# A hybrid encoder block on one core: both mixer projections with tokens stationary, some of their blocks by seven products instead of eight

## The chip, the core and the metric

The kernel runs on one core of a Trainium2 chip. The core has a matrix engine (TensorE, PE in the rows, with weight loads PEld), a vector engine (VectorE, DVE), a scalar engine (ScalarE, ACT), a general engine (GpSimd, POOL) and a sync engine (SyncE, SP) that here only issues DMAs. Each engine takes its instructions in program order. The metric is the device time of one execution in microseconds, the median of several.

## The reference

256 tokens of width 4096 go through two sub-layers, in fp32. Cut to what matters:

```python
h = rmsnorm(x, g_pre)
proj = h @ w_in                                   # 4096 x 12288
q, k, v, gate_a, u_b, gate_b = split(proj)        # widths 2048 each
y_a = chunked_rel_attention(q, k, v) * silu(gate_a)          # 16 heads of 128
y_b = multiscale_pool(u_b, w_pool, pool_scale) * silu(gate_b)  # 4 groups of 512
x = x + rmsnorm(concat(y_a, y_b) @ w_out, g_post)            # 4096 x 4096
h = rmsnorm(x, g_xa_pre); m = rmsnorm(mem, g_mem)            # 256 memory tokens
q, k, v = h @ w_xq, m @ w_xk, m @ w_xv            # widths 1024, 4 heads of 256
x = x + rmsnorm(softmax(q @ k.T) @ v @ w_xo, g_xa_post)
```

`w_in` and `w_out` are three quarters and one quarter of the mixer's weights, 256 MB in fp32, and by far the most of the arithmetic.

## The kernel before, in words

**Precision.** Every fp32 operand is split in two fp32r parts, a high part (a rounded copy) and a low part (the difference). A product is made of three: high by high, low by high, high by low.

**The stream.** All weights come in one list of *subs* (`stream_order`, L43), tiles of 128 partitions x 1024 columns in fp32, 512 KB each. `load_sub` (L155) brings a sub into one of 4 `raw` buffers. `split_sub` (L162) makes its high part with a copy on ACT (L174) and its low part with a subtraction on DVE (L175), into one of 4 ring buffers. The main loop (L939) takes one sub per iteration *i*, which this document calls slot *i*: first the steps listed for the slot's start, then `split_sub` of sub i+3, the DMA of sub i+7, the other steps listed for the slot (`at(i, f)` puts f there), then the matmuls of sub *i*. So everything is issued in the order of this list, on each engine's own queue, and a step that waits holds up all that stands behind it on its engine.

**Two forms of matmul.** In *column form* (`mm_cols`, L274, lines L277 and L278) a 128 x 128 block of weights is stationary and the 256 tokens move: one matmul of 512 columns (high and low tokens side by side) with the high weights, one of 256 with the low weights. The result has features on partitions. In *strip form* (`mm_strip`, L280, lines L286 to L288) 128 tokens are stationary and 512 weight columns move: three matmuls of 512 for each half of the tokens, with tokens on partitions in the result. Before the change v (a quarter of the columns of group A) and the cross-attention's v are in strip form; q, k, both gates, the pool input and w_out are in column form; the cross-attention's k (`mm_xk`, L290) is in column form with 256 moving columns.

**Around the matmuls.** The first 16 slots also build xHL, the split input (`x_prep`, L321). A column result is gathered from PSUM by a copy on ACT and an addition on DVE (L298). For each head there are steps at set slots after the end of its k columns: `head_qk_split`, `head_scores`, `head_max`, `head_exp`, `head_soft`, `head_turn` (transposes on PE, L414), `head_turned`, `head_att`, `head_y`. The gates use an exponential on ACT and a reciprocal on DVE. There are 8 PSUM banks; a product in progress holds one, a v strip two. PE is given its next sub as soon as both parts of it are there.

The DMA queue of SP carries all weights; PSUM banks are taken and given back in a fixed order by `bank` and `done` (L119, L125).

Of the kernel before, what the change touches and what calls it, by code (L numbers as in the profile page):

```python
# [36 lines left out]
XV_REST = 24  # L37
XO_HEAD = 6
OUT_HEAD = 4
# [3 lines left out]
def stream_order():  # L43
# [14 lines left out]
    subs = []  # L58
    for hg in range(4):
        subs += [strip("v", hg, k) for k in range(0, KT, 2)]  # L60
        for h in range(4 * hg, 4 * hg + 4):
            for c in (h, 16 + h, 48 + h):
                subs += cols("in", c)
    xv = [strip("xv", 0, k) for k in range(0, KT, 2)]
    for g in range(4):
        for j, c in enumerate([64 + 4 * g + j for j in range(4)] + [80 + 4 * g + j for j in range(4)]):
            subs += cols("in", c)
            if j % 2 if g else j == 7:
                subs.append(xv.pop(0))
        if g < 3:  # L70
            subs += pool(g)
    subs += xv
    for k in (0, 4):
        for c in range(0, OUT_HEAD, 2):
            subs += [[("out", c + j, k + i) for j in range(2) for i in range(4)]]
    for k in range(8, KT, 8):
        if k == 16:
            subs += pool(3)
        subs += [[("out", c, k + i) for i in range(8)] for c in range(OUT_HEAD)]
    for c in range(OUT_HEAD, KT):  # L80
        subs += cols("out", c)
    for k in range(0, KT, 2):
        subs += [[("xk", k)], [("xk", k + 1)]]
        if k < XV_REST:
            subs += [strip("xv", 1, k)]
    for c in range(8):
        subs += cols("xq", c)
    subs += [strip("xv", 1, k) for k in range(XV_REST, KT, 2)]
    for k in (0, 4):
        for c in range(0, XO_HEAD, 2):  # L90
            subs += [[("xo", c + j, k + i) for j in range(2) for i in range(4)]]
    for c in range(XO_HEAD, KT):
        subs += [[("xo", c, i) for i in range(8)]]
    return subs
# [3 lines left out]
def block_kernel(ctx: ExitStack, tc: tile.TileContext, x, mem, ws, relb, vecs, out):  # L98
    nc = tc.nc
    subs = stream_order()  # L100
    n = len(subs)
    LA = 3
    WB = LA + 1
    RAWB = 4
    XB = 3
# [3 lines left out]
    big = ctx.enter_context(tc.tile_pool(name="big", bufs=1))  # L109
    wpool = ctx.enter_context(tc.tile_pool(name="wpool", bufs=1))  # L110
    xin = ctx.enter_context(tc.tile_pool(name="xin", bufs=XB))
    com = ctx.enter_context(tc.tile_pool(name="com", bufs=1))
    psum = ctx.enter_context(tc.tile_pool(name="psum", bufs=1, space=bass.MemoryType.PSUM))
# [26 lines left out]
    def halves(name):  # L140
        t = [big.tile([P, 16, 512], F32R, tag=f"A{j}", name=f"{name}{j}") for j in range(2)]

        def part(kt, k=1):
            return t[kt // 16][:, kt % 16:kt % 16 + k, :]

        return part

    def pairs(ap):
        return ap.rearrange("p (a b) -> p a b", b=S)


    raws, Hs, Ls = {}, {}, {}
    held = {}

# [6 lines left out]

    def split_sub(s, cuts=1):  # L162
        if s >= n:
            return
        r = raws.pop(s)
        if s in held:
            h, l = held[s]()
        else:
            h = wpool.tile([P, SUB], F32R, tag="wh", name="wh", bufs=WB)
            l = wpool.tile([P, SUB], F32R, tag="wl", name="wl", bufs=WB)  # L170
        w = SUB // cuts
        for j in range(cuts):
            c = slice(j * w, j * w + w)
            nc.scalar.copy(h[:, c], r[:, c])  # L174
            nc.vector.tensor_sub(l[:, c], r[:, c], h[:, c].bitcast(F32))  # L175
        Hs[s], Ls[s] = h, l

    def load_x(src, c, store, tag, eng=None):
        store[c] = xin.tile([P, 2, S], F32, tag=tag, name=tag, bufs=XB)
        (eng or nc.sync).dma_start(store[c], src[c])  # L180

    def split_act(dst, src, g):

        nc.scalar.activation(dst[:, :S], src, AF.Copy, scale=g)
        nc.vector.scalar_tensor_tensor(dst[:, S:], src, g, dst[:, :S].bitcast(F32), op0=OP.mult, op1=OP.subtract)


    class Rms:


        def __init__(self, name):
            self.name = name
            self.acc = None

        def square(self, src):

            if self.acc is None:
                self.acc = buf("acc", [P, 2, S], f"acc_{self.name}")
                nc.scalar.activation(self.acc, src, AF.Square)
                self.sq = None  # L200
            else:
                self.sq = buf("sq", [P, 2, S], "sq", bufs=2)[:, :src.shape[1], :]
                nc.scalar.activation(self.sq, src, AF.Square)

        def add(self):
            if self.sq is not None:
                nc.vector.tensor_add(self.acc, self.acc, self.sq)
                self.sq = None

        def sums(self, src=None, first=True, last=True):  # L210
            if first:
                self.p = bank("ms")
            src = self.acc if src is None else src
            for t in range(2):
                for j in range(src.shape[1]):
                    nc.tensor.matmul(self.p[:, t:t + 1], src[:, j, t * P:(t + 1) * P], ones[:, 0:1],
                                     start=first and t + j == 0, stop=last and j == src.shape[1] - 1,
                                     skip_group_check=True)

        def root(self):  # L220
            v = const.tile([P, 2], F32, name=f"v_{self.name}")
            nc.vector.tensor_scalar(v, self.p[:, 0:2], 1.0 / D, EPS, op0=OP.mult, op1=OP.add)
            done(self.p)
            self.r = const.tile([P, 2], F32, name=f"r_{self.name}")
            nc.gpsimd.tensor_tensor(out=self.r, in0=v, in1=half, op=OP.pow)
            self.dg = buf("dg", [P, 2, P], "dg")
            nc.vector.tensor_mul(self.dg, ident[:, None, :].to_broadcast([P, 2, P]),
                                 self.r[:, :, None].to_broadcast([P, 2, P]))

        def spread(self):  # L230
            self.q = bank("mr")
            nc.tensor.matmul(self.q[:, :S], ones, self.dg.rearrange("p a b -> p (a b)"), start=True, stop=True)

        def keep(self):
            self.R = buf("R", [P, S], f"R_{self.name}", bufs=2)
            nc.scalar.copy(self.R, self.q[:, :S])
            done(self.q)

        def all_at(self, i):
# [3 lines left out]
            at(i + 2, self.spread)  # L243
            first_at(i + 3, self.keep)


    class HalfRms:
# [5 lines left out]
        def sums(self, src, first, last):  # L253
            if first:
                self.p = bank("ms")
            for j in range(src.shape[1]):
                nc.tensor.matmul(self.p[:, 0:1], src[:, j, :], ones[:, 0:1], start=first and j == 0,
                                 stop=last and j == src.shape[1] - 1, skip_group_check=True)

        def root(self):  # L260
            v = const.tile([P, 1], F32, name=f"v_{self.name}")
            nc.vector.tensor_scalar(v, self.p[:, 0:1], 1.0 / D, EPS, op0=OP.mult, op1=OP.add)
# [3 lines left out]
            self.dg = buf("dg", [P, 2, P], "dg")[:, 0, :]  # L266
            nc.vector.tensor_scalar(self.dg, ident, r[:, 0:1], None, op0=OP.mult)

        def spread(self):
            self.q = bank("mr")  # L270
            nc.tensor.matmul(self.q[:, :P], ones, self.dg, start=True, stop=True)


    def mm_cols(acc, H, L, kk, X, first, last):  # L274

        w = slice(kk * P, kk * P + P)
        nc.tensor.matmul(acc, H[:, w], X, start=first, stop=last, skip_group_check=True)  # L277
        nc.tensor.matmul(acc[:, :S], L[:, w], X[:, :S], start=False, stop=last, skip_group_check=True)  # L278

    def mm_strip(accs, H, L, kk, X, first, last):  # L280

        w = slice(kk * 512, kk * 512 + 512)
        for t in range(2):
            xh = X[:, t * P:(t + 1) * P]
            xl = X[:, S + t * P:S + (t + 1) * P]
            nc.tensor.matmul(accs[t], xh, H[:, w], start=first, stop=False)  # L286
            nc.tensor.matmul(accs[t], xl, H[:, w], start=False, stop=False)  # L287
            nc.tensor.matmul(accs[t], xh, L[:, w], start=False, stop=last)  # L288

    def mm_xk(accs, H, L, X, first, last):  # L290
        for j in range(8):
            o = accs[j // 2][:, (j % 2) * S:(j % 2) * S + S]
            w = slice(j * P, j * P + P)
            nc.tensor.matmul(o, H[:, w], X[:, :S], start=first and j % 2 == 0, stop=False, skip_group_check=True)  # L294
            nc.tensor.matmul(o, H[:, w], X[:, S:], start=False, stop=False, skip_group_check=True)  # L295
            nc.tensor.matmul(o, L[:, w], X[:, :S], start=False, stop=last, skip_group_check=True)  # L296

    def gather(acc, dst):  # L298

        t = buf("t1", [P, S], "t1", bufs=2)  # L300
        nc.scalar.copy(t, acc[:, S:])  # L301
        nc.vector.tensor_add(dst, acc[:, :S], t)
        done(acc)

    accs = {}
    where = {}
    for i, s in enumerate(subs):
        for t in s:
# [8 lines left out]

# [713 lines left out]
```

## Time and profile before

| | |
|---|---|
| median of 3 runs | 1890.54 us (1890.3 to 1892.93) |
| the profiled execution | 1891.73 us |
| its span, first to last instruction | 1889.9 us |
| mean granted TensorE clock | 0.995 |
| busy: PE, DVE, ACT | 1868.0, 1221.1, 896.5 us |
| weights and inputs moved | 366.83 MB, 194 GB/s |

The sum of a profile is made against the profiled execution's own time, 1891.73, of which 1889.9 lie between its first and last instruction. A timeline row gives the start of an instruction, its length, the engine, the line, and what it writes and reads; the length of one matmul is longer than the distance to the next, since they are pipelined, so the distance of starts is the price. The same holds for DVE and ACT in a smaller measure. In square brackets stands how long the engine was idle before, and what it waited for.

### The profile page before, as it was taken

To read this page: it belongs to the slowest core of one execution; us is meant where nothing else is said; L and a number is where in the kernel's file an instruction comes from. 1 tells how busy PE (TensorE), PEld (TensorE's weight loads), DVE (VectorE), ACT (ScalarE), POOL (GpSimd) and SP (SyncE) were. 2 spreads that over 40 slices of the span, in tenths; PEclk is the share of its full clock that TensorE was granted. 3 is DMA by queue.
4 is the path that set the end of the run, shared out by engine and by line. 5 is a ranking of instruction groups with operands and counts; after the bars stand their busy time and mean duration, and the time that the engine had idled before them with its cause. 6 is when DMAs were issued, how large, how long until landed. Compare 5 with 4: busy or idle time off the path is not lost.

```text
span 1889.9 us, 27452 instructions
## 1 busy us (share of the span) xinstructions
PE 1868.0 (99%) x10732; PEld 1633.7 (86%) x10732; DVE 1221.1 (65%) x1654; ACT 896.5 (47%) x1277; POOL 11.2 (1%) x16
## 2 busy tenths in 40 slices
PE   9999999999999999999999999999999999999995
PEld 7888888888888888888888888888888899988885
DVE  8566556655665666585867678755555569955686
ACT  8444444444444444444444446544444456634551
POOL 0000000000000000000000000000000000000001
PEclk9999999999999999999999999999999999999997
DMA  8555555555555555556655556555555567755452
GB/s 303 197 195 184 188 190 191 183 190 189 185 186 192 188 184 188 184 184 211 200 201 195 192 196 209 189 190 192 190 190 190 191 232 253 243 177 181 165 190 90
DMA packets 114226, 366.83 MB, mean 194 GB/s; under 512 B 11952, under 2 KB 22320, under 8 KB 114096
## 3 DMA queue, kind: packets, MB, share of 16 engines
q1 hardware_dynamic: 111328, 363.50, 57.9%
q8 instruction: 84, 1.38, 0.3%
q10 hardware_dynamic: 2768, 1.57, 0.3%
q14 instruction: 46, 0.38, 0.1%
HBM read 360.83 MB, written 4.19 MB: 193 GB/s over the span
## 4 chain that ended last, share of the span: by engine, by line
PE 98%; DVE 1%; DMA 0%; ACT 0%; POOL 0%; issue 0%; ACTq 0%; SPq 0%; DVEq 0%; POOLq 0%
PE acc L277 50%; PE acc L278 25%; PE va L288 2%; PE va L286 2%; PE vb L286 2%; PE vb L287 2%; PE vb L288 2%; PE va L287 2%; PE xk L294 2%; PE xk L296 2%; PE xk L295 2%; PE acc L884 1%; DVE y L834 0%; PE xs L671 0%; PE xat L713 0%; DVE y L840 0%
## 5 line engine op out<-in xcount | busy, mean ns | idle before, releaser
L175 DVE TENSOR_TENSOR wl<-raw,wh 128x1024 fp32r<-128x1024 f32 (+1 forms) x645 | 788.5, 1223 | 634.6 <-ACT wh L174 633.5
L174 ACT CAST wh<-raw 128x1024 fp32r<-128x1024 f32 (+1 forms) x645 | 676.8, 1049 | 912.0 <-PE acc L277 652.1
L277 PE MATMUL acc<-xHL,wh 128*128 128x512 f32 x2560 | 900.5, 397 | 0.0
L278 PE MATMUL acc<-xHL,wl 128*128 128x256 f32 x2560 | 714.9, 279 | 0.0
L277 PEld LDWEIGHTS acc<-xHL,wh 128*128 128x128 f32 x2560 | 481.1, 188 | 112.9
L278 PEld LDWEIGHTS acc<-xHL,wl 128*128 128x128 f32 x2560 | 482.8, 189 | 0.6
L277 PE MATMUL acc<-yHL,wh 128*128 128x512 f32 x1024 | 355.5, 394 | 0.0
L278 PE MATMUL acc<-yHL,wl 128*128 128x256 f32 x1024 | 283.9, 277 | 0.0
L277 PEld LDWEIGHTS acc<-yHL,wh 128*128 128x128 f32 x1024 | 192.1, 188 | 44.7
L278 PEld LDWEIGHTS acc<-yHL,wl 128*128 128x128 f32 x1024 | 192.4, 188 | 0.1
L277 PE MATMUL acc<-h2HL,wh 128*128 128x512 f32 x256 | 91.2, 401 | 0.0
L294 PE MATMUL xk<-mhl,wh 128*128 128x256 f32 x256 | 72.5, 283 | 0.0
L296 PE MATMUL xk<-mhl,wl 128*128 128x256 f32 x256 | 72.2, 282 | 0.0
L295 PE MATMUL xk<-mhl,wh 128*128 128x256 f32 x256 | 72.1, 282 | 0.0
L278 PE MATMUL acc<-h2HL,wl 128*128 128x256 f32 x256 | 71.6, 280 | 0.0
L277 PE MATMUL acc<-xoHL,wh 128*128 128x512 f32 x192 | 67.0, 395 | 0.0
L301 ACT COPY t<-acc 128x256 f32<-128x256 f32 x160 | 57.2, 364 | 3.6 <-PE acc L278 3.6
L277 PEld LDWEIGHTS acc<-h2HL,wh 128*128 128x128 f32 x256 | 48.1, 188 | 11.4
L447 DVE RECIPROCAL ge<-ge 128x256 f32<-128x256 f32 x32 | 56.1, 1753 | 1.1
L278 PE MATMUL acc<-xoHL,wl 128*128 128x256 f32 x192 | 53.3, 277 | 0.0
L286 PE MATMUL va<-wh,xHL 128*128 128x512 f32 x128 | 51.0, 398 | 0.5 <-ACT wh L174 0.4
L288 PE MATMUL va<-wl,xHL 128*128 128x512 f32 x128 | 50.2, 392 | 0.5 <-DVE wl L175 0.5
(202 smaller groups left out, 1804.2 us busy)
## 6 DMA issues: line engine op xcount, KB each, us to landing
raw<-ws_dram SPq DMA_DIRECT2D x647, 512.0 KB, 3.3
min<-mem_dram SPq DMA_DIRECT2D x36, 256.0 KB, 3.7
xin<-x_dram SPq DMA_DIRECT2D x31, 256.0 KB, 3.9
rb<-relb_dram SPq DMA_DIRECT2D x16, 192.0 KB, 3.5
out_dram<-y SPq DMA_DIRECT2D x3, 512.0 KB, 3.0
out_dram<-y SPq DMA_DIRECT2D x4, 256.0 KB, 3.0
out_dram<-y ACTq DMA_DIRECT2D x3, 256.0 KB, 2.2
raw<-ws_dram SPq DMA_DIRECT2D x2, 256.0 KB, 4.7
```

Source lines behind the costliest of these rows:

```text
L174: nc.scalar.copy(h[:, c], r[:, c])
L175: nc.vector.tensor_sub(l[:, c], r[:, c], h[:, c].bitcast(F32))
L277: nc.tensor.matmul(acc, H[:, w], X, start=first, stop=last, skip_group_check=True)
L278: nc.tensor.matmul(acc[:, :S], L[:, w], X[:, :S], start=False, stop=last, skip_group_check=True)
L286: nc.tensor.matmul(accs[t], xh, H[:, w], start=first, stop=False)
L287: nc.tensor.matmul(accs[t], xl, H[:, w], start=False, stop=False)
L288: nc.tensor.matmul(accs[t], xh, L[:, w], start=False, stop=last)
L294: nc.tensor.matmul(o, H[:, w], X[:, :S], start=first and j % 2 == 0, stop=False, skip_group_check=True)
L295: nc.tensor.matmul(o, H[:, w], X[:, S:], start=False, stop=False, skip_group_check=True)
L296: nc.tensor.matmul(o, L[:, w], X[:, :S], start=False, stop=last, skip_group_check=True)
L301: nc.scalar.copy(t, acc[:, S:])
L447: nc.vector.reciprocal(e, e)
```

## The change

**Pairs and quads.** All of w_in and w_out is now computed with tokens stationary. A *pair* is two strips of 512 columns: A0 to A3 (v and gate of a head group), B0 to B3 (q and k), U0 to U3 (pool input and gate) and O0 to O3 (w_out). The stream runs A0, B0, A1, B1, ..., U0 to U3, O0 to O3. A *quad* is two k tiles of 128 by the two strips, two subs; a pair has 16 quads, 32 slots. Slots 0 to 31 are A0, 32 to 63 B0, 64 to 95 A1.

**Seven products.** In a quad the four token blocks (two halves of the tokens by two k tiles) and the four weight blocks of 128 x 512 form a 2 x 2 block product, 8 block products of 3 matmuls, 24 in all. In 6 of the 16 quads of each pair but A0, B0 and O0 (`FAST`, `DIRECT`) it is done with seven block products of sums and differences, 21 matmuls. The weight differences (T3, b12-b11, T2, T4) are made on DVE for each such quad; the token sums are made once, by `x_forms` for w_in and `y_forms` for w_out. The seven results stay in PSUM over a pair, in seven banks P1 to P7, and are put together at its end by `early`, `late1` and `late2`. Direct quads of such a pair add into the same banks.

**Turning.** Results now have tokens on partitions. Those which must have features there (both gates, q, k, pool input, w_out's output) are turned by `turn`, 4 transposes on PE and a copy on ACT.

**Also.** The ring has 5 buffers instead of 4. x is read twice: once in the first 16 slots for A0, and again for `x_forms`, at slots 19 to 41. The mixer's output goes out to DRAM by `y_store` and comes back for `y_forms`. Gates use a tanh instead of exponential and reciprocal. xk is in strip form with turned results, the first half of xv is computed beside it, the second after xq. The statistics of w_out's output are made by ACT with an accumulating square. The tail's moving operands are copied to contiguous tiles first.

The diff's core:

```diff
+PAIRS = ([p for g in range(4) for p in (("A", g), ("B", g))] + [("U", g) for g in range(4)]
+         + [("O", m) for m in range(4)])
+DIRECT = (("A", 0), ("B", 0), ("O", 0))
+FAST = (4, 6, 8, 10, 12, 14)
...
-    WB = LA + 1
+    WB = 5
...
+    def piece(src, cuts=1, to=None):
...
+            A.copy(h[:, c], src[:, c])
+            V.tensor_sub(l[:, c], src[:, c], h[:, c].bitcast(F32))
+        return h, l
...
     def split_sub(s, cuts=1):
-        if s >= n:
+        while waiting:
+            waiting.pop(0)()
+        if s >= n or (fast(s) and meta[s][2] == 0):
             return
...
+        r1, r2 = raws.pop(s - 1), raws.pop(s)
+        b11, b12, b21, b22 = r1[:, :512], r1[:, 512:], r2[:, :512], r2[:, 512:]
+        t3, t2, t4 = tt[:, 0:512], tt[:, 512:1024], tt[:, 1024:1536]
+        V.tensor_sub(t3, b22, b12)
+        V.tensor_sub(b12, b12, b11)
+        w = Hs[s - 1] = {}
+        w["b2"] = piece(r2)
+        w["b1"] = piece(r1)
+        V.tensor_sub(t2, b22, b12)
+        V.tensor_sub(t4, b21, t2)
+
+        def rest():
+            w["t3"] = piece(tt[:, 0:1024])
+            w["t4"] = piece(t4)
+        waiting.append(rest)
...
+    def mm_block(acc, xs, w, first, last):
+
+        T_.matmul(acc, xs[0], w[0], start=first, stop=False)
+        T_.matmul(acc, xs[1], w[0], start=False, stop=False)
+        T_.matmul(acc, xs[0], w[1], start=False, stop=last)
...
+        if o in FAST:
+            if half == 0:
+                return (("P2", "A12", ("b2", 0)), ("P3", "S4", ("b2", 1)), ("P1", "A11", ("b1", 0)),
+                        ("P5", "S1", ("b1", 1)))
+            return ("P7", "S3", ("t3", 0)), ("P6", "S2", ("t3", 1)), ("P4", "A22", ("t4", 0))
...
+    def turn(pair, k, dst, scale=1.0):
+
+        src, p = result(pair)[k], bank("tn")
+        for c in range(4):
+            T_.transpose(p[:, c * P:(c + 1) * P], src[:, c * P:(c + 1) * P], ident)
...
+    def x_forms(c):
+        src = xch.pop((1, c))
...
+            V.scalar_tensor_tensor(ft[:, a:b, :], tiles(src[:, j, :]), gv[:, G_MIX_PRE + k:G_MIX_PRE + k + 1], R,
+                                   op0=OP.mult, op1=OP.mult)
...
+        if c in FAST:
+            sums_of(ft[:, 6, :], ft[:, 7, :], ft[:, 0, :], ft[:, 1, :], ft[:, 2:6, :])
+        else:
+            q = ft[:, :6, :].rearrange("p (k f) b -> p k f b", f=3)
+            V.tensor_sub(q[:, :, 2, :], q[:, :, 0, :], q[:, :, 1, :])
+        split_copy(h, l, ft[:, :u, :])
...
+        i = first + (3 * c) // 2
+        at(i - 3, load_x, c, 1)
+        at(i, x_forms, c)
...
+        e = end_slot["A", hg]
+        at(e + 2, a_gates, hg)
+        at(e + 3, a_keep, hg)
+        e = end_slot["B", hg]
+        at(e + 1, b_turn, hg, 0)
+        at(e + 2, b_turn, hg, 1)
+        for j in range(4):
+            h, o = 4 * hg + j, e + 4 + 7 * j
+            at(o - 3, head_bias, h)
+            at(o - 1, head_qk_split, h)
+            at(o, head_scores, h)
+            first_at(o + 1, head_max, h)
+            at(o + 2, head_exp, h)
+            at(o + 3, head_soft, h)
+            at(o + 5, head_turn, h)
+            at(o + 6, head_turned, h)
+            at(o + 8, head_att, h)
+            at(o + 9, head_y, h)
```

In the rows of instructions below, a row is the line, the operation, what it writes and reads, and the size; x2 means twice in a row. `wl` and `wh` are low and high parts of weights, `tt` holds T2 to T4, `ahl` and `aql` the split keys, probabilities and queries of a head, `x_80` and `x_81` scratch tiles (probabilities, bias), `sc` scores, `ft` the token forms, `e_u_73` and `e_u_74` two results of a pair.

DVE around the scores of a head, before (the head's k and q are split between two weight tiles):

```order
L355 TENSOR_TENSOR qk<-t_778,R_x 128x256
L175 TENSOR_TENSOR wl<-raw,wh 128x1024
L338 TENSOR_TENSOR ahl<-qk,ahl 128x256
L338 TENSOR_TENSOR ahl<-qk,ahl 128x128
L175 TENSOR_TENSOR wl<-raw,wh 128x1024 x3
L391 SCALAR_TENSOR_TENSOR pr<-sc,rb 128x384
```

DVE at the same step of the second head, in the second pair A1, after (slots 74 to 76):

```order
L204 TENSOR_TENSOR tt<-raw 128x512
L205 TENSOR_TENSOR raw<-raw 128x512
L186 TENSOR_TENSOR wl<-raw,wh 128x1024 x2
L209 TENSOR_TENSOR tt<-raw 128x512
L210 TENSOR_TENSOR tt<-raw,tt 128x512
L225 TENSOR_TENSOR ahl<-pt,ahl 128x256
L225 TENSOR_TENSOR ahl<-k,ahl 128x256
L225 TENSOR_TENSOR aql<-q,aql 128x128
L186 TENSOR_TENSOR wl<-tt,wh 128x1024
L186 TENSOR_TENSOR wl<-tt,wh 128x512
L186 TENSOR_TENSOR wl<-raw,wh 128x1024
```

The split of the head's operands now stands behind all the differences and two of the pieces of a coming fast quad.

DVE after the first results, before (the split of v lies between weight tiles):

```order
L227 TENSOR_TENSOR dg<-ident,r_x 128x256
L175 TENSOR_TENSOR wl<-raw,wh 128x1024 x4
L338 TENSOR_TENSOR vhl<-v,vhl 128x512
L175 TENSOR_TENSOR wl<-raw,wh 128x1024
L302 TENSOR_TENSOR t_684<-acc,t_685 128x256
```

DVE at slots 33 and 34, after:

```order
L186 TENSOR_TENSOR wl<-raw,wh 128x1024 x2
L550 SCALAR_TENSOR_TENSOR ft<-tt,gv,x_80 128x256 x2
L398 TENSOR_TENSOR ft<-ft 128x128
L399 TENSOR_TENSOR ft<-ft 128x128
L400 TENSOR_TENSOR ft<-ft 128x128
L401 TENSOR_TENSOR ft<-ft 128x128
L225 TENSOR_TENSOR Fa_77<-ft,Fa_77 128x896
L225 TENSOR_TENSOR extra<-ft,extra 128x128
L510 SCALAR_TENSOR_TENSOR e_u_73<-x_80,e_u_73 128x512
L510 SCALAR_TENSOR_TENSOR e_u_74<-x_80,e_u_74 128x512
```

The last two rows are the gates of A0, which PE turns at slot 35; a fast form of x stands directly ahead of them.

PE at the same head's scores, before:

```order
L277 MATMUL acc<-xHL_115,wh 128x512
L278 MATMUL acc<-xHL_115,wl 128x256
L383 MATMUL sc<-qk 128x128
L376 MATMUL sc<-ahl 128x256
L377 MATMUL sc<-ahl 128x256
L378 MATMUL sc<-ahl 128x256
L277 MATMUL acc<-xHL_115,wh 128x512
```

PE at slots 74 and 75, after:

```order
L321 MATMUL P_1596<-wh,Fb_79 128x512
L322 MATMUL P_1596<-wh,Fb_79 128x512
L323 MATMUL P_1596<-wl,Fb_79 128x512
L621 MATMUL sc<-k,q 128x128
L615 MATMUL sc<-ahl,aql 128x256
L616 MATMUL sc<-ahl,aql 128x256
L617 MATMUL sc<-ahl,aql 128x256
L321 MATMUL P_1584<-wh,Fb_79 128x512
```

The four matmuls of the scores stand between the products of two subs, as before; the products are now three matmuls of 512 per bank.

## Rows read from the trace of the kernel before

**Rows 1.** The page: busy time and instructions by engine; then the chain by line.

```profile
PE 1868.0 (99%) x10732; PEld 1633.7 (86%) x10732; DVE 1221.1 (65%) x1654; ACT 896.5 (47%) x1277; POOL 11.2 (1%) x16
...
PE acc L277 50%; PE acc L278 25%; PE va L288 2%; PE va L286 2%; PE vb L286 2%; PE vb L287 2%; PE vb L288 2%; PE va L287 2%; PE xk L294 2%; PE xk L296 2%; PE xk L295 2%; PE acc L884 1%; DVE y L834 0%; PE xs L671 0%; PE xat L713 0%; DVE y L840 0%
```

**Rows 2.** Groups by form: line engine op names shapes, busy us, mean ns, idle before.

```profile
L277 PE MATMUL acc<-xHL,wh 128*128 128x512 f32 x2560 | 900.5, 397 | 0.0
...
L277 PE MATMUL acc<-yHL,wh 128*128 128x512 f32 x1024 | 355.5, 394 | 0.0
```

**Rows 3.** Timeline of PE, two stretches of column matmuls of w_in.

```profile
100.24 0.40 PE L277 MATMUL acc<-xHL,wh 128*128 128x512 f32 x1
...
105.79 0.40 PE L277 MATMUL acc<-xHL,wh 128*128 128x512 f32 x1
...
299.92 0.40 PE L277 MATMUL acc<-xHL,wh 128*128 128x512 f32 x1
...
300.98 0.40 PE L277 MATMUL acc<-xHL,wh 128*128 128x512 f32 x1
```

**Rows 4.** Timeline of PE, strip form, one slot of twelve matmuls apart.

```profile
590.07 0.39 PE L286 MATMUL va<-wh,xHL 128*128 128x512 f32 x1
...
592.79 0.39 PE L286 MATMUL va<-wh,xHL 128*128 128x512 f32 x1
```

**Rows 5.** Timeline of PE, xk, three matmuls apart.

```profile
1600.03 0.28 PE L294 MATMUL xk<-mhl,wh 128*128 128x256 f32 x1
...
1600.39 0.28 PE L294 MATMUL xk<-mhl,wh 128*128 128x256 f32 x1
```

**Rows 6.** Timeline of PE, the transposes of one head and the matmuls behind.

```profile
98.18 0.49 PE L414 MATMUL pt<-ident,pr 128*128 128x128 f32 x3
98.43 0.47 PE L277 MATMUL acc<-xHL,wh 128*128 128x512 f32 x1
98.74 0.28 PE L278 MATMUL acc<-xHL,wl 128*128 128x256 f32 x1
```

**Rows 7.** Groups by form: the weight tiles on DVE and ACT.

```profile
L175 DVE TENSOR_TENSOR wl<-raw,wh 128x1024 fp32r<-128x1024 f32 x643 | 787.1, 1225 | 632.8 <-ACT wh L174 631.7
...
L174 ACT CAST wh<-raw 128x1024 fp32r<-128x1024 f32 x643 | 675.6, 1051 | 910.2 <-PE acc L277 652.1 <-issue 116.8 <-PE vb L287 104.1
```

**Rows 8.** Timeline of DVE while it has no wait.

```profile
33.93 0.69 DVE L207 TENSOR_TENSOR acc_x<-acc_x,sq 128x512 f32<-128x512 f32 x1
34.53 0.88 DVE L185 SCALAR_TENSOR_TENSOR xHL<-xin,gv,xHL 128x256 fp32r<-128x256 f32 x2
35.33 1.22 DVE L175 TENSOR_TENSOR wl<-raw,wh 128x1024 fp32r<-128x1024 f32 x1
36.46 0.69 DVE L207 TENSOR_TENSOR acc_x<-acc_x,sq 128x512 f32<-128x512 f32 x1
```

**Rows 9.** Timeline of ACT and DVE: hand-offs between the engines.

```profile
590.04 1.05 ACT L174 CAST wh<-raw 128x1024 fp32r<-128x1024 f32 x1 [1.67 <-PE vb L287]
...
101.37 1.05 ACT L174 CAST wh<-raw 128x1024 fp32r<-128x1024 f32 x1 [1.75 <-PE acc L277]
...
102.45 1.23 DVE L175 TENSOR_TENSOR wl<-raw,wh 128x1024 fp32r<-128x1024 f32 x1 [0.24 <-ACT wh L174]
103.60 0.42 DVE L338 TENSOR_TENSOR ahl<-pt,ahl 128x256 fp32r<-128x256 f32 x1
...
104.05 0.27 ACT L420 COPY ptc<-pt 128x128 f32<-128x128 f32 x1 [1.36 <-DVE ahl L338]
```

**Rows 10.** Windows near the end: us, PE busy (matmuls), PEclk, DMA share, GB/s.

```profile
1867.00:1868.00 1.00, 0.89 (x8) 1.00 0.00 0
1868.00:1869.00 1.00, 0.00 (x0) 1.00 0.59 179
1869.00:1869.50 0.50, 0.00 (x0) 1.00 1.14 346
...
1870.00:1870.50 0.50, 0.00 (x0) 0.50 0.05 11
```

More of the change, by code (lines that the diff above doesn't have):

```diff
@@ L72, in stream_order, with put @@
[L72 to L81, printed above, removed]
+    subs, meta = [], []
+    def put(new):
+        subs.extend(new)
+        meta.extend([None] * len(new))
@@ L82, in stream_order @@
+    for i, pair in enumerate(PAIRS):
+        kind = "out" if pair[0] == "O" else "in"
+        n1, n2 = strips(pair)
+        for o in range(QUADS):
+            if o == LEAD and i and PAIRS[i - 1][0] == "U":
+                put(pool(PAIRS[i - 1][1]))
+            for half in range(2):
+                subs.append([(kind, c, 2 * o + half) for c in n1 + n2])
+                meta.append((pair, o, half))
     for k in range(0, KT, 2):
-        subs += [[("xk", k)], [("xk", k + 1)]]
-        if k < XV_REST:
-            subs += [strip("xv", 1, k)]
+        put([[("xk", k)], [("xk", k + 1)], strip("xv", 0, k)])
@@ L162, in split_sub, with fast @@
+    def fast(s):
+        m = s < n and meta[s]
+        return m and m[0] not in DIRECT and m[1] in FAST
     def split_sub(s, cuts=1):
-        if s >= n:
+        while waiting:
+            waiting.pop(0)()
+        if s >= n or (fast(s) and meta[s][2] == 0):
             return
[L165 to L180, printed above, removed]
-    def split_act(dst, src, g):
-        nc.scalar.activation(dst[:, :S], src, AF.Copy, scale=g)
-        nc.vector.scalar_tensor_tensor(dst[:, S:], src, g, dst[:, :S].bitcast(F32), op0=OP.mult, op1=OP.subtract)
+        if not fast(s):
+            Hs[s], Ls[s] = piece(raws.pop(s), cuts, held.get(s))
+            return
@@ L205, in add, with sums @@
         def add(self):
             if self.sq is not None:
-                nc.vector.tensor_add(self.acc, self.acc, self.sq)
+                a = pairs(self.acc)
+                V.tensor_add(a, a, self.sq)
                 self.sq = None
[L210 to L213, printed above, removed]
+        def sums(self):
+            self.p = bank("ms")
+            src = pairs(self.acc)
@@ L214, in sums @@
             for t in range(2):
[L215 to L220, printed above, removed]
+                for j in range(2):
+                    T_.matmul(self.p[:, t:t + 1], src[:, j, tok(t)], ones[:, 0:1], start=t + j == 0, stop=j == 1,
+                              skip_group_check=True)
@@ L290, in mm_xk @@
[L290 to L302, printed above, removed]
+        T_.matmul(acc, H[:, w], X, start=first, stop=last, skip_group_check=True)
@@ new lines, in block_kernel, with mm_pair @@
+    left = {}
+    for pair in PAIRS:
+        for o in range(QUADS):
+            for half in range(2):
+                for k, _, _ in products(pair, o, half):
+                    left[pair, k] = left.get((pair, k), 0) + 1
+    open_banks = {}
+    def mm_pair(i):
+        pair, o, half = meta[i]
+        if fast(i):
+            w = Hs[i - half]
+            if half:
+                del Hs[i - half]
+        else:
+            w = Hs.pop(i), Ls.pop(i)
+        for k, xname, wn in products(pair, o, half):
+            key = pair, k
+            start = key not in open_banks
+            if start:
+                open_banks[key] = bank(k)
+            left[key] -= 1
+            if fast(i):
+                h, l = w[wn[0]]
+                wn = wn[1]
+            else:
+                h, l = w
+            c = slice(512 * wn, 512 * wn + 512)
+            mm_block(open_banks[key], unit(pair, o, half, xname), (h[:, c], l[:, c]), start, left[key] == 0)
@@ new lines, in block_kernel @@
+    for g in range(4):
+        e = end_slot["U", g]
+        at(e + 1, pool_u, g)
+        i = [e + 2, e + 4]
+        for b in range(2):
+            for j in range(g + 1):
+                at(i[b], pool_sum, g, b, j)
+            at(i[b] + 1, pool_d, g, b)
+        at(e + 6, pool_gates, g)
+        at(e + 7, pool_turn, g)
+        for c in range(4):
+            j = end("pool", g, c)
+            at(j + 1 + c % 2, pool_y, g, c)
+            at(j + 3 + c % 2, y_store, 16 + 4 * g + c, "sg", c)
@@ new lines, in block_kernel, with x2, o_turn, o_sq @@
+    for c in range(QUADS):
+        i = slot[("O", 0), c, 0] - 3
+        at(i - 4, load_y, c)
+        at(i, y_forms, c)
+    x2t = []
+    ssq = const.tile([P, 2, 8], F32, name="ssq")
+    def x2(k, m=1):
+        return x2t[k // 4][:, k % 4:k % 4 + m, :]
+    def o_turn(m, s):
+        if m == 0 and s == 0:
+            x2t.extend(buf(f"X{j}", [P, 4, S], f"x2_{j}") for j in range(8))
+        for t in range(2):
+            turn(("O", m), f"c{t + 1}{s + 1}", x2t[2 * m + s][:, :, tok(t)])
+    def o_sq(m, s):
+        for t in range(2):
+            b = result(("O", m))[f"c{t + 1}{s + 1}"]
+            A.activation(b, b, AF.Square, accum_out=ssq[:, t, 2 * m + s:2 * m + s + 1])
```

846 lines of the change are left out of this document (485 added, 361 removed).

## Prediction

> **What bounds the kernel now.** I read the page first, then stretches of TensorE's (PE) timeline, then what VectorE (DVE) and ScalarE (ACT) take for one weight tile, and last the end of the program. PE is busy for 1868.0 of 1889.9 us, and three quarters of the chain that ended last lie in its two column-form lines L277 and L278; DVE is busy for 65% and ACT for 47% [rows 1]. So a matmul fewer is time saved for as long as DVE and ACT keep up, and any wait that the change puts before PE is time lost. DVE and ACT sit waiting today: ACT's copies wait for PE to give ring buffers back, DVE's subtractions wait for ACT [rows 7]. That slack, about 1.5 us in each 2.72 us slot, is what the change spends.
>
> The profiled execution took 1891.73 us, its span 1889.9. I make the sum on it and subtract 1.2 us at the end, since the median of the runs is 1890.54.
>
> **What PE saves.** A column unit (128 of k by 128 columns) is one 512-wide and one 256-wide matmul. Sixteen units run from 100.24 to 105.79 us, 0.347 each; three near a head's work from 299.92 to 300.98, 0.353 [rows 3]; w_in has both kinds, w_out, with little beside it, I take at 0.347. In token-stationary form twelve matmuls of 512 run from 590.07 to 592.79, 0.2267 each [rows 4]. The column units number 2560 for w_in and 1024 for w_out [rows 2], and v has 768 strip matmuls (4 strips of 32 k tiles, 6 each). Today that work takes 2560 x 0.350 + 1024 x 0.347 + 768 x 0.2267 = 1425 us. After it there are 16 pairs x 16 quads x 24 = 6144 matmuls, less 3 in each of 78 fast quads (13 pairs x 6): 5910, x 0.2267 = 1340. **-85 us**: the 234 that fall away are 53 of it, the change of form 32. Bounds: -64 if the new matmuls run at 0.229, which a busier DVE and ACT could bring, and all columns at 0.347; -93 with the columns of w_in at 0.353.
>
> xk goes from 768 matmuls of 256 at 0.12 (three in 0.36, [rows 5]), 92 us, to 384 of 512 at 0.2267, 87: **-4** (0 to -5). The tail's contiguous operands I cost at nothing.
>
> **What PE gets on top.** 56 turned results and 4 of xk need 4 transposes each, 240. Three of today's take 98.18 to 98.43, and the matmul behind them takes 0.31 instead of 0.23 [rows 6]: 0.33 per three, and (4 x 0.083 + 0.08) = 0.41 per four, 60 x 0.41 = **+25** (20 to 30).
>
> So PE alone would come to 1889.9 - 85 - 4 + 25 = 1826. The rest is waits that do not exist today.
>
> **Weight preparation of a fast quad.** DVE issues a 512-wide operation every 0.60, a 1024-wide one every 1.13 and two scaled subtractions of 256 in 0.80 [rows 8]. A fast quad needs four differences of 512 and pieces of 1024, 1024, 1024 and 512: 4 x 0.60 + 3 x 1.13 + 0.60 = 6.4 us, where a direct quad needs 2.26. A fast and a direct quad together: 8.7 us of DVE for 45 matmuls, 10.2 us of PE. Alone this fits, and I cost it at nothing. The 1.5 us of cover is gone wherever DVE has something else to do; the next four terms are those places.
>
> **x_forms, +11.** x is read again and built into forms at slots 19 to 41, one every 1.5 slots, while A0 and B0 run direct. A plain form takes 0.80 (two scalings), 0.33 (a 256 subtraction), then DVE stands still until ACT has copied 768 columns (about 0.9 with the hand-off: copy to subtraction is 1.08 for 1024, [rows 9]), then 0.87: 3.0. A fast form takes 3.9 (four more 128-wide sums). Iterations 19 to 33 hold 7 plain and 3 fast forms and 15 pieces: 21 + 11.7 + 17 = 49.7 us against 15 x 2.72 = 40.8 of PE: DVE falls 8.9 behind. In iteration 34 the gates of A0 (two 512-wide operations) stand behind a piece and a fast form, 6.3 us. With five ring buffers DVE starts iteration 19 about 1.3 us after PE starts slot 18. So the gates end 1.3 + 8.9 + 6.3 = 16.5 us after PE would start slot 33; PE wants to turn them at slot 35, 5.4 after it. Queued behind that turn are all the matmuls of slot 35. Wait: 11 (2 if ACT's copies cost DVE nothing, 14 with wider hand-offs). Later pieces are in time again.
>
> **Attention in the fast zone, +37.** The work of a head group runs during the next pair, four times (A1, A2, A3, U0) across its fast quads, on in-order queues. Seven banks are held by products, so scores, transposes and outputs of a head share the eighth. I count from PE's start of the first fast quad in A1. PE would end its next three slots at 2.7, 5.1 and 7.8, and then do head 1's scores. DVE's piece for the slot of the scores can begin only when PE gives a ring buffer back in the first slot: ACT at 1.3, DVE 2.4 to 3.5 [rows 9]. Then come two differences, two pieces, two differences, to 8.3, and only behind them the low halves of k, q and the transposed probabilities, each after an ACT copy that itself waits for DVE (1.4 us of such waiting stands between DVE and ACT today already, in the last of rows 9): 9.9 instead of 8.2, wait 1.7. Then head 0's output waits for head 1's maximum, which frees the bank; the maximum stands behind a piece whose buffer PE gives back at the end of the slot before: ACT 12.7, DVE 13.8 to 15.0, maximum 15.5, PE free at 12.8: 2.8. By the same count head 1's output waits 2.4 behind T4, head 3's scores 2.2, the rest under 0.3 each. 9.1 per pair, x 4 = **+37**. Bounds: 4 per pair if only the two outputs wait, a little less each, 13 if each of the eight scores and outputs waits: 16 to 52.
>
> **Pool and y_forms, +10.** In U1, U2 and U3 three banks of the fast quads become free only after pool_y of the group before, about 2 us each: +6 (0 to 9). In O0 the sums of the last pool group and 16 y_forms (DVE 1.9 to 3.4 per two slots) come on top of the pieces; pool_turn waits behind them: +4 (0 to 10). The y stores and loads through DRAM are 256 KB each on SP's queue between weight loads; the load stands four slots ahead of its use, I cost it at nothing.
>
> **The sum.** 1889.9 - 85 - 4 + 25 + 11 + 37 + 6 + 4 = 1884 of span, with 1.8 around it 1885.7, less 1.2: **1884 us**, 0.3% below today's median.
>
> **Rivals.**
> - *The waits are absorbed.* A wait of PE gives DVE that time to catch up, so the next is shorter; for it speaks that DVE has 1.5 us per quad pair to spare, against it that each wait above starts from a buffer PE itself returns late, so being ahead does not help. With 3 for x_forms, 16 for attention and 5 for the pools: 1884 - 34 = 1850.
> - *The clock falls in the waits.* Today PE hardly stops and the granted clock is 1.00. The one long stop shows what follows: the last matmul of the tail's stream ends before 1868, the clock is 1.00 up to 1869.5, and 0.50 from 1870, that is 1.2 GHz [rows 10]. The waits of 11 us at slot 35 and of 2.2 to 2.8 in the attention pairs are of the length after which it fell there. If the slot behind each of the 17 runs at the lower level, it takes up to 2.72 more: 46, of which DVE's catching up gives half back: +20, 1904. From 10 us in all on the change is slower. The Trainium skill (TensorE: Matmul & The Clock Gate, section "HAM oscillation — how this bites in real kernels") says that a kernel whose matmul bursts are parted by waits is throttled again in each wait and starts every burst at the lower clock; the drop at the end of this trace agrees, but nothing here shows whether a 2 us wait is enough.
> - *The one spare bank makes all eight attention steps wait.* 13 per pair, and the pools and O0 at their upper ends: 1884 + 15 + 9 + 3 = 1911. By itself it turns the result from 11.6 per pair on. For it speaks that only one bank is left; against it that half of the steps fall in direct quads.
> - *Nothing moves.* What the seven products save goes to the waits to the microsecond: 1887 to 1894.
>
> **How the numbers follow.** The forecast holds with 0.40 (most of it faster, a part within the bound), the absorbed waits 0.18, the clock 0.22, the bank 0.14, no change 0.06. About 0.2% is what a measurement of this kernel can tell from no change, that is 1887 to 1894. Faster: 0.18 + 0.32 = 0.50; same 0.08 + 0.06 = 0.14; slower 0.36. The range reaches from the absorbed case, 1850, to just past the bank case, 1914; beyond it lie PE's bare 1826 and clock and bank together. The likeliest case by itself spans 1874 to 1894.
>
> **What would show it.** Matmuls of L321 to L323 0.227 apart and 5910 of them; a PE wait of about 11 us near 100 us on the gates' line; in each of A1, A2, A3 and U0 four waits of 1.7 to 2.8 us on the low halves and on the maximum; PE idle some 60 us in all and a granted clock of 1.00. A granted clock below 0.98 speaks for the second rival, more than 12 us of waits per attention pair for the third, fewer than 6 for the first. I am wrong at the root if the fast quads stall without any attention beside them (A2 to A3's later slots, or O1 to O3): then the weight differences are the bound, not what comes on top.

## The result, and the profile after

The changed kernel takes **1932.57 us** (1931.96 to 1936.49) against 1890.72 before (the median of four runs; the 1890.54 above is of the first three): a ratio of 1.0223, 95% interval 1.0206 to 1.0241. The forecast was 1884, the range 1850 to 1914. It is slower, not faster, and outside the range. The profiled execution took 1932.26 us, its span 1930.3: 40.4 us more than before, 46 more than the forecast's span of 1884.

The page of the changed kernel: busy time by engine, the chain by engine, and the weight work of the fast quads on ACT and DVE.

```profile
PE 1843.5 (96%) x8552; PEld 1528.7 (79%) x8552; DVE 1507.4 (78%) x2023; ACT 1039.5 (54%) x1433; POOL 12.3 (1%) x17
...
PE 82%; DVE 10%; ACT 4%; issue 3%; DMA 1%; POOL 0%; SPq 0%; ACTq 0%; DVEq 0%; POOLq 0%
...
L185 ACT CAST wh<-tt 128x1024 fp32r<-128x1024 f32 (+1 forms) x156 | 123.4, 833 | 152.3 <-DVE tt L209 138.6
L186 DVE TENSOR_TENSOR wl<-tt,wh 128x1024 fp32r<-128x1024 f32 (+1 forms) x156 | 143.1, 955 | 37.6 <-ACT wh L185 36.7
```

Beside [rows 1]: PE has 2180 instructions fewer, but it now stands still at times; 18% of the chain lies outside PE's rows (DVE 10%, ACT 4%, issue 3%, DMA 1%). DVE has 286 us more to do.

The list of PE's waits: what it waited for, us in total, times, the longest. `c` and `P` are the result banks of direct and of fast pairs, `tn` a result being turned, `at` a head's output.

```profile
PE at L615 <- DVE x L630: 20.9, 8, 2.8
PE tn L499 <- DVE e_u L510: 20.2, 7, 12.3
PE sc L621 <- ACT x L659: 13.1, 8, 1.7
PE ms L296 <- DVE tt L1109: 5.8, 1, 5.8
PE P L321 <- DVE x L333: 5.1, 6, 1.3
```

These are the waits of the prediction: outputs of heads behind the maximum (L630), A0's gates (L510, one of 12.3), scores behind the split of the head's operands, banks behind pool_y (L333). The fourth row is the tail's, which was 5.6 before. Nothing stalls where no attention stands beside the fast quads: from 479 to 615 us, from 670 to 806 us and in O1 to O3 no wait is longer than 0.4 us.

The granted clock is where the traces part. Its mean over the span of the changed kernel:

```profile
core 0: 1930.3 us, clock 0.979
```

It was 0.995 before, and below 0.98 stood in the prediction as the sign of its second rival. Windows of PE in A1, ahead of the head's waits and at them (us, PE busy and matmuls, PEclk, DMA share, GB/s):

```profile
224.00:232.00 8.00, 8.00 (x38) 1.00 0.41 143
232.00:240.00 8.00, 6.32 (x22) 0.79 0.42 158
240.00:250.00 10.00, 7.23 (x22) 0.66 0.15 54
```

And the timeline of PE around the first of these waits (start, length, what, idle before):

```profile
233.09 0.39 PE L323 MATMUL P<-wl,Fb 128*128 128x512 f32 x1
235.14 0.49 PE L621 MATMUL sc<-k,q 128*128 128x128 f32 x2 [1.67 <-ACT x L659]
...
236.48 0.63 PE L321 MATMUL P<-wh,Fb 128*128 128x512 f32 x1
236.91 0.63 PE L322 MATMUL P<-wh,Fb 128*128 128x512 f32 x1
237.34 0.63 PE L323 MATMUL P<-wl,Fb 128*128 128x512 f32 x1
...
239.75 0.39 PE L323 MATMUL P<-wl,Fb 128*128 128x512 f32 x1
239.98 0.39 PE L321 MATMUL P<-wh,Fb 128*128 128x512 f32 x1
240.21 0.40 PE L322 MATMUL P<-wh,Fb 128*128 128x512 f32 x1
```

After a wait of 1.67 us the matmuls start 0.43 us apart, nearly twice the 0.227 of [rows 4], and then 0.23 again. That is the lower level, 1.2 GHz. In the kernel before, the clock fell only once, at the end of the program [rows 10]; here it also falls at 14 places ahead of that: behind 11 of the 16 long waits of the attention, in the wait of 12.3 us, and twice behind the turns of the pool's gates (waits of 1.4 and 0.7 us in a row, and of 4.5 us).

**Where 40.4 us come from**, summed over the starts of all PE instructions of both traces, waits taken out:

| | forecast | measured |
|---|---|---|
| weight matmuls, at the full clock | -89 | -80 |
| transposes and other small matmuls | +25 | +31 |
| waits of PE | +58 | +64 |
| matmuls at the lower clock | 0 | +24 |
| sum | -6 | +40 |

The sum is 39.7 before rounding; the other 0.7 us lie behind the last matmul. The clock's row is 95 weight matmuls 0.4288 apart instead of 0.2292 (19 us) and some 50 small ones (5 us). The first three rows came out 9, 6 and 6 us worse than forecast.

### The profile page after: what moved, and what is told of

Read it like the earlier page. It is cut to its first block, busy times and chain, and to the rows that moved or that the text cites. A ratio compares the mean times of both kernels' runs of the same rounds, so it can differ in the third digit from the quotient of the medians.

```text
span 1930.3 us, 24141 instructions
## 1 busy us (share of the span) xinstructions
PE 1843.5 (96%) x8552; PEld 1528.7 (79%) x8552; DVE 1507.4 (78%) x2023; ACT 1039.5 (54%) x1433; POOL 12.3 (1%) x17
## 4 chain that ended last, share of the span: by engine, by line
PE 82%; DVE 10%; ACT 4%; issue 3%; DMA 1%; POOL 0%; SPq 0%; ACTq 0%; DVEq 0%; POOLq 0%
PE P L321 16%; PE P L322 16%; PE P L323 16%; PE acc L316 6%; DVE wl L186 4%; PE c L321 4%; PE c L323 4%; PE c L322 4%; PE acc L317 3%; ACT wh L185 3%; PE xv L323 1%; PE xv L322 1%; PE xv L321 1%; PE tn L499 1%; PE xk L321 1%
## 5 line engine op out<-in xcount | busy, mean ns | idle before, releaser
L321 PE MATMUL P<-wh,Fa 128*128 128x512 f32 x938 | 372.7, 397 | 5.4 <-DVE x L333 5.1
L322 PE MATMUL P<-wh,Fa 128*128 128x512 f32 x938 | 368.8, 393 | 0.0
L323 PE MATMUL P<-wl,Fa 128*128 128x512 f32 x938 | 368.0, 392 | 0.0
L321 PE MATMUL P<-wh,Fb 128*128 128x512 f32 x588 | 234.6, 399 | 0.0
L323 PE MATMUL P<-wl,Fb 128*128 128x512 f32 x588 | 232.1, 395 | 0.0
L322 PE MATMUL P<-wh,Fb 128*128 128x512 f32 x588 | 231.9, 394 | 0.0
L321 PEld LDWEIGHTS P<-wh,Fa 128*128 128x128 f32 x938 | 178.8, 191 | 44.9 <-issue 6.7
L323 PEld LDWEIGHTS P<-wl,Fa 128*128 128x128 f32 x938 | 178.3, 190 | 38.1
L322 PEld LDWEIGHTS P<-wh,Fa 128*128 128x128 f32 x938 | 178.5, 190 | 35.7
L185 ACT CAST wh<-tt 128x1024 fp32r<-128x1024 f32 (+1 forms) x156 | 123.4, 833 | 152.3 <-DVE tt L209 138.6
L186 DVE TENSOR_TENSOR wl<-tt,wh 128x1024 fp32r<-128x1024 f32 (+1 forms) x156 | 143.1, 955 | 37.6 <-ACT wh L185 36.7
L322 PEld LDWEIGHTS P<-wh,Fb 128*128 128x128 f32 x588 | 112.5, 191 | 22.6
L321 PEld LDWEIGHTS P<-wh,Fb 128*128 128x128 f32 x588 | 112.6, 191 | 22.5
L321 PE MATMUL c<-wh,Fa 128*128 128x512 f32 x276 | 107.9, 391 | 1.8 <-ACT wh L185 1.8
L322 PE MATMUL c<-wh,Fa 128*128 128x512 f32 x276 | 107.4, 389 | 0.0
```

What stands on the lines that cost most here:

```text
L185: A.copy(h[:, c], src[:, c])
L186: V.tensor_sub(l[:, c], src[:, c], h[:, c].bitcast(F32))
L321: T_.matmul(acc, xs[0], w[0], start=first, stop=False)
L322: T_.matmul(acc, xs[1], w[0], start=False, stop=False)
L323: T_.matmul(acc, xs[0], w[1], start=False, stop=last)
```

## Experiments

Theory A: the waits come from where a step stands on DVE's queue, and the lower clock follows from the waits. Rival B: DVE is full in the fast zone, and a wait taken away in one place comes back in another. Rival C: the lower clock has another cause, or costs nothing, since PE waits anyway. From e5 on the expectations say A2: theory A, with DVE short of time only in single stretches (around x_forms and the fourth head). All times are medians; before ran at 1890.5 to 1891.3 beside them.

### Does the clock cost anything by itself?

```diff
+    def fill(i, k):
+        p = next(b for (pair, _), b in open_banks.items() if pair == meta[i][0])
+        for _ in range(k):
+            T_.matmul(p, zero, forms["Fb1"][:, :512], start=False, stop=False, skip_group_check=True)
...
+        if hg == 0:
+            at(e + 3, fill, e + 3, 48)
...
+            if j % 2:
+                at(o, fill, o, 6)
...
+            if j < 2:
+                at(o + 8, fill, o + 8, (11, 10)[j])
```

> The order of after, with matmuls that add zero put in front of the waiting ones: 48 before the turn of A0's gates, 6 or 11 before the scores and outputs that wait in A1, A2, A3 and U0, 180 in all, 41 us of extra work for PE in stretches in which it waited; the results do not change. Theory A: PE never stands still there for long, the granted clock stays at 1.00, and the time falls by what the lower clock cost, 15 to 22: 1911 to 1918, in spite of the extra work. Rival C (the lower clock has another cause, or costs nothing since PE waits anyway): the time stays at 1932 or rises.

Measured (e3): **1912.39**, 20 us less than after (ratio to before 1.0114, 1.0097 to 1.0131), with 180 matmuls more. Windows of PE in this kernel, the same place as above:

```profile
224.00:232.00 8.00, 8.00 (x37) 1.00 0.36 116
232.00:240.00 8.00, 7.72 (x35) 1.00 0.51 182
240.00:250.00 10.00, 9.79 (x46) 1.00 0.33 105
```

PE is busy with work that adds nothing, the clock stays at 1.00 at every place that was filled, and the program is faster. By the starts of PE's instructions the added matmuls cost 45 us, the waits are 41 less, and the price of the lower clock falls from 24 to 3. What is left of it stands behind the turns of two pool gates, which were not filled. So C falls: the lower clock is a price of standing still, on top of the waits, and 20 us come back without taking away a single dependency.

### Are the attention waits a matter of order?

```diff
-            at(o - 1, head_qk_split, h)
-            at(o, head_scores, h)
-            first_at(o + 1, head_max, h)
+            first_at(o - 1, head_qk_split, h)
+            first_at(o, head_scores, h)
+            first_at(o, head_max, h)
...
-            at(o + 6, head_turned, h)
+            first_at(o + 6, head_turned, h)
```

> Theory A (order and clock): the attention waits come only from where the head steps stand on DVE's queue, and the lower clock follows from the waits. With the split of k and q, the split of the turned probabilities and the maximum put ahead of the weight work of their slot, the 16 waits of 1.6 to 2.8 us (34 us) go, and with them the stretches at the lower clock behind them (some 15 us): 1932.6 - 34 - 15 = 1884, between 1875 and 1895. Rival B (DVE is the bound in the fast zone): the weight work is then late instead, PE waits for wl and wh at L321 and L323, and the time stays above 1915.

Measured (e1): **1892.32** (ratio 1.0011, 1.0001 to 1.002): 40 less than after, 8 more than expected. By the starts, 23 of the 40 are waits and about 14 the lower clock. In slots 64 on to the end of the heads' work PE's waits are now these:

```profile
PE sc L621 <- ACT x L659: 10.6, 4, 2.7
PE P L323 <- DVE wl L186: 1.8, 4, 0.5
PE tn L499 <- DVE e_u L492: 1.4, 1, 1.4
```

The eight waits on the maximum are gone, and so are four of the eight on the scores. Mostly A, but the other four, one per pair at the fourth head's scores, have grown from 1.6 to 2.7. DVE, ACT and PE there, from the trace of this kernel:

```profile
268.79 2.57 DVE L186 TENSOR_TENSOR wl<-raw,wh 128x1024 fp32r<-128x1024 f32 x2
271.27 0.69 DVE L209 TENSOR_TENSOR tt<-raw 128x512 f32<-128x512 f32 x1
271.99 0.69 DVE L210 TENSOR_TENSOR tt<-raw,tt 128x512 f32<-128x512 f32 x1
273.16 1.82 DVE L186 TENSOR_TENSOR wl<-tt,wh 128x1024 fp32r<-128x1024 f32 x2 [0.47 <-ACT wh L185]
274.90 1.22 DVE L186 TENSOR_TENSOR wl<-raw,wh 128x1024 fp32r<-128x1024 f32 x1
276.04 0.42 DVE L225 TENSOR_TENSOR ahl<-pt,ahl 128x256 fp32r<-128x256 f32 x1
...
276.49 0.27 ACT L659 COPY x<-pt 128x128 f32<-128x128 f32 x1 [1.63 <-DVE ahl L225]
...
276.80 0.49 PE L621 MATMUL sc<-k,q 128*128 128x128 f32 x2 [2.65 <-ACT x L659]
```

PE has been waiting since 274.2 for the bank that the copy at L659 empties; DVE has not been idle for more than half a microsecond and is still at weights. At this one place B is right.

### The gates of A0: the step or the stretch?

```diff
-        at(e + 2, a_gates, hg)
-        at(e + 3, a_keep, hg)
+        g = 14 if hg == 0 else 2
+        at(e + g, a_gates, hg)
+        at(e + g + 1, a_keep, hg)
```

> The gates of A0 and their turns move from slots 34 and 35 to slots 46 and 47, behind the last x_forms. Theory A: the one wait of 12.3 us goes, and the lower clock behind it (about 3 us): 1932.6 - 15 = 1917, no other wait in its place. Rival B: DVE is behind by then with the pieces too, so most of the wait comes back at a weight tile or at the later turn: 1928 or more.

Measured (e2): **1929.47** (1.0205, 1.019 to 1.022). B: most of the wait did not go, it came back in pieces. PE's waits from 100 to 150 us in this kernel:

```profile
PE c L323 <- DVE wl L186: 4.9, 9, 0.6
PE c L321 <- ACT wh L185: 2.8, 5, 0.8
```

So the stretch is short of DVE time, as the forecast's own sum said (49.7 us in 40.8). The other way is to stretch it:

```diff
-        i = first + (3 * c) // 2
+        i = first + 2 * c
```

> x_forms one every 2 slots (19 to 49) instead of every 1.5; the gates stay at slots 34 and 35. Moving the gates later left the time where it was, since the waits came back at the weight pieces, 0.5 us at a time. Theory A2 (capacity in this stretch: 49.7 us of DVE work in 40.8 of PE's): at 2 slots DVE has 5.3 to 6.2 us of work in 5.4, it no longer falls behind, and the gate wait shrinks to under 2 with no waits at pieces in its place: 1932.6 - 10.5 - 3 = 1919, between 1914 and 1924. Rival (the gate step itself is too close to its turn, whatever DVE did before): the wait stays above 6 and the time above 1924.

Measured (e5): **1921.01** (1.0162, 1.0147 to 1.0177). PE's waits from 95 to 150 us:

```profile
PE tn L499 <- DVE e_u L510: 2.4, 2, 2.0
```

12.3 has become 2.0, with nothing in its place.

### What are the seven products worth?

```diff
-DIRECT = (("A", 0), ("B", 0), ("O", 0))
-FAST = (4, 6, 8, 10, 12, 14)
+DIRECT = tuple(PAIRS)
+FAST = ()
```

> All pairs direct, no seven-product quads, no weight differences, plain token forms only; everything else as in after. Theory A: PE does 234 matmuls more, 53 us; the attention waits (34), part of the gate wait (5), the waits at the pools (about 6) and the lower clock (about 20) go: 1932.6 + 53 - 65 = 1920, between 1910 and 1932, so that the seven products as they stand bring nothing. If the fast quads were worth their matmuls in after, this would be 1960 to 1985.

Measured (e4): **1906.89** (1.0086, 1.0071 to 1.0101), 26 less than after and 13 below what I expected. With 234 matmuls fewer the kernel is slower than with them. Even all direct it is slower than the kernel before: by the starts, the weight matmuls are 26 us shorter, the small ones (mostly the turns) 22 longer, and the waits 18 longer, 9.6 of them at A0's gates.

The same question in an order with few waits. First the order (e6: the head steps as above, x_forms every 2 slots, the fourth head one slot later), then the pool's matmuls a quad earlier and its gates three slots earlier (e7), then e7 with all pairs direct (e8). e6 has one more move: the turns of the gates of A1 to A3 come a slot later, where neither e1 nor e6 shows a wait of PE; the store of the fourth head's output stays in its slot. Of the cut below the lines of `h, o`, `a_keep` and `y_store` are new in e6, the others in e7.

```diff
-        at(e + 3, a_keep, hg)
+        at(e + 3 + (hg > 0), a_keep, hg)
...
-            h, o = 4 * hg + j, e + 4 + 7 * j
+            h, o = 4 * hg + j, e + 4 + 7 * j + (j == 3)
...
-            at(o + 11 if j < 3 else o + 10, y_store, h, "sg", j)
+            at(o + 11 if j < 3 else o + 9, y_store, h, "sg", j)
...
-LEAD = 4
+LEAD = 3
...
-        at(e + 6, pool_gates, g)
-        at(e + 7, pool_turn, g)
+        at(e + 3, pool_gates, g)
+        at(e + 5, pool_turn, g)
```

> Three changes of order together: the head steps ahead of the weight work (as in the first experiment), x_forms every 2 slots, and the fourth head of a group one slot later, since its scores waited 2.65 us there for DVE, which had no idle time ahead of them. Theory A2: 1892.3 - 13 (gate) - 10.6 (scores of the fourth head) - 7 (lower clock behind them) = 1862, between 1855 and 1872. Rival B (DVE is full in the whole fast zone with attention): the wait of the fourth head moves by a slot and stays over 1.5 us, time above 1872.

> As e6, and the pool: its matmuls one quad earlier, its gates at the 3rd and their turns at the 5th slot of the next pair instead of the 6th and 7th. Theory A2: of the waits left (pool banks 5, turns of the pool's gates 7, about 12 in all) 8 or more go, with little of the clock: e6 less 8 to 12, about 1852. If the steps only wait in another place, it equals e6 within 3 us.

> The order of e7 with all pairs direct and plain forms, so 234 matmuls more and no weight differences. Against e7 it measures what the seven products are worth where little waits: theory A2 says most of the 53 us of PE, 35 to 50, so about 1852 + 40 = 1892 (1885 to 1902). If DVE's load costs what the products save even then, it lies within 10 us of e7.

Measured: e6 **1886.0** (0.9973, 0.9961 to 0.9984), e7 **1877.85** (0.994, 0.9924 to 0.9957), e8 **1895.07** (1.0022, 1.0013 to 1.0032). e6 misses its 1862 by 24: the fourth head's wait did not go with the one slot (B). It spread over four instructions in a row, 2.8 to 3.8 us in all where 2.7 stood in e1, and the lower clock still follows. PE's waits in the heads' stretch of e6:

```profile
PE at L615 <- DVE x L630: 5.0, 5, 1.7
PE sc L615 <- ACT aql L224: 3.8, 4, 1.0
PE sc L616 <- DVE ahl L225: 2.8, 4, 0.7
PE sc L621 <- ACT x L659: 2.0, 4, 0.5
```

e7 comes 8 below e6, as A2 had it. e8 against e7: the seven products are worth 17 us here, not 35 to 50. DVE and PE busy in e7 and, below it, in e8:

```profile
PE 1826.0 (97%) x8552; PEld 1519.8 (81%) x8552; DVE 1507.2 (80%) x2023; ACT 1041.3 (56%) x1433; POOL 12.3 (1%) x17
```

```profile
PE 1862.3 (98%) x8786; PEld 1558.5 (82%) x8786; DVE 1104.8 (58%) x1407; ACT 940.3 (50%) x1304; POOL 12.3 (1%) x17
```

Over the starts of all PE instructions e7 saves 45 us of weight matmuls against e8 and gives back 17 in waits and 9 in small matmuls (what the lower clock costs is inside these). For 53 us of PE at most, DVE pays 402.

### One fast quad fewer where DVE is full

```diff
-FAST = (4, 6, 8, 10, 12, 14)
+FAST = (4, 6, 8, 10, 14)
```

Both kernels have the pool's matmuls back at the fifth quad (`LEAD = 4`); e9 has no other change against e7. Quad 12 is the fifth entry of the list.

> As e7, with the pool's matmuls back at the fifth quad and its gates still early. In e7 the pool's matmuls themselves waited (1.0, 2.5 and 3.7 us) for the sums on DVE. Theory A2: these 7 us go, the waits of three banks come back (about 1.7 in each of U1 to U3, 5 us), the two long ones with their lower clock do not: e7 less 2 to 6, 1872 to 1876.

> As e9, with five fast quads in a pair instead of six: the seventh quad of the list (12) is direct, the one whose differences DVE makes just ahead of the fourth head's scores. 39 matmuls more, 8.8 us. Theory A2 (DVE is full around the fourth head, and only there): the 2.8 to 3.7 us that PE waits there in each of A1, A2, A3 and U0 go (13 us), and the lower clock behind them (4 to 8): 1874 + 9 - 19 = 1864, between 1858 and 1871. If DVE is full in the whole zone (B), the waits only move and the time rises to 1878 to 1884.

Measured: e9 **1876.0** (0.9917, 0.9903 to 0.9932), e10 **1863.74** (0.9857, 0.9841 to 0.9874). e9 is 2 below e7, at the edge of what was expected. From e9 to e10, 39 matmuls more take 12 us off, where 10 were expected; the mean granted clock rises from 0.988 to 0.994, and PE's waits in the heads' stretch of e10 are these:

```profile
PE at L615 <- DVE x L630: 3.0, 4, 1.1
PE P L323 <- DVE wl L186: 1.9, 4, 0.5
PE P L321 <- DVE x L333: 1.7, 2, 1.4
```

In e9 no other place of that stretch shows a wait over 0.6 us. So DVE is full around the fourth head and not in the whole zone. No run left out another quad instead, so what an equal cut elsewhere would bring is not shown. e10 is 69 us below the changed kernel and 27 below the one before.

## Why the prediction was wrong

- **The waits were right.** Forecast 1.7, 2.8, 2.4 and 2.2 in an attention pair, measured 1.66, 2.76, 2.46 and 1.62 (A2 to U0), 34 us in all four pairs against 37; the gate wait 11 against 12.3. The places and the instructions that ended them are those named. DVE at the second head in A1 of the changed kernel shows the order that the prediction counted through:

```profile
231.90 1.22 DVE L186 TENSOR_TENSOR wl<-raw,wh 128x1024 fp32r<-128x1024 f32 x1
233.05 0.68 DVE L209 TENSOR_TENSOR tt<-raw 128x512 f32<-128x512 f32 x1
233.76 0.69 DVE L210 TENSOR_TENSOR tt<-raw,tt 128x512 f32<-128x512 f32 x1
234.37 0.42 DVE L225 TENSOR_TENSOR ahl<-pt,ahl 128x256 fp32r<-128x256 f32 x1
235.43 0.43 DVE L225 TENSOR_TENSOR ahl<-k,ahl 128x256 fp32r<-128x256 f32 x1 [0.64 <-ACT ahl L224]
...
241.76 1.23 DVE L186 TENSOR_TENSOR wl<-raw,wh 128x1024 fp32r<-128x1024 f32 x1 [3.37 <-ACT wh L185]
242.91 0.55 DVE L630 SCALAR_TENSOR_TENSOR x<-sc,x 128x384 f32<-128x384 f32 x1
...
243.60 0.55 PE L615 MATMUL at<-ahl,vs 128*128 128x256 f32 x1 [2.77 <-DVE x L630]
```

  The last three rows are the wait on the maximum (L630): DVE stood idle for 3.37 us ahead of the weight piece at the head of its queue, so this wait is one of order and not of a full engine.

- **The step that failed is the clock.** The forecast carried 17 long waits and at the same time a granted clock of 1.00, and left the drop to a rival with 0.22, "nothing here shows whether a 2 us wait is enough". [rows 10] showed the level fall behind PE's last matmul, and the prediction itself called its waits of 11 and of 2.2 to 2.8 us long enough for that. Once they were counted, the term belonged in the sum. Its price was given as 20; 24 were measured, and 20 us came back when the waits were filled (e3). The Trainium skill ("TensorE: Matmul & The Clock Gate", section "HAM oscillation — how this bites in real kernels") says that matmul bursts parted by waits each start again at the lower clock; the trace agrees behind 11 of the 16 attention waits, with 0.43 us a matmul where 0.227 stood, and not behind the other five.
- **The matmuls came out 9 us dearer.** Most start 0.227 apart, as taken, but 85 that stand directly ahead of a small matmul or behind one take 0.31 to 0.42 each, 10 us in all above 0.227. The prediction had counted that join for the transposes alone.
- **The small matmuls came out 6 us dearer, the waits 6 as well.** The attention's waits were 3 less than forecast, others more: the pool's last gate waited 4.5 in O0, where 4 stood for all of it, and the turns of U1's and U2's gates, 0.7 to 1.4 each, were not in the sum.
- **The range** took each bound by itself. With the measured 24 of the clock alone the forecast would have been 1908, slower than before and still inside the range; the 21 us of the three small misses lie in the same direction and carried it past 1914. No single rival held them together.
- **The first rival, absorbed waits, fell**: the attention's waits did not shrink from one pair to the next. The reason given against it, that a wait starts from a buffer which PE itself returns late, fits the wait on the maximum above; for the others it is argued and not shown.
- **Two slips in the sums** change nothing. The figures for xk, 92 to 87, give -5 and not -4 (measured 91.8 to 87.4). The bank rival's 1911 holds 3 us for which no term is named; 1884 + 15 + 9 is 1908.
- What stays open is why a wait of 2.4 or 1.6 us is followed by the lower clock in one place and not in another (none behind the second output of A1, nor behind the fourth head's scores). The length of the wait alone does not decide it: in e5 the lower level follows the fourth head's scores in A1 and A2, after 1.6 us, and does not follow the first output of A2, after 2.8. No run took that apart.

## What to carry to other kernels

When the bound engine has been busy without a break, a change that cuts its work and makes it wait must be charged twice: for the wait, and for the lower clock that can follow it (here 64 and 24 us). Saved matmuls paid for with work of the next-busiest engine are worth what is left after that engine's fullest stretch: here 53 us of products gave a loss of 26 in one order, a gain of 17 in another, and dropping one of the six fast quads of a pair, where DVE was full, gained 12. Put the small steps that PE waits for ahead of the bulk work on an in-order queue before looking for fewer operations.

## What was not expected of the hardware

Eleven of sixteen waits of 1.6 to 2.8 us were followed by matmuls 0.43 instead of 0.227 us apart; with 180 useless matmuls in the waits the clock stayed at 1.00 at the places that were filled, and the program was 20 us faster.
